# A decoder layer on one core: the opening loads in one queue, ten block pairs instead of eleven with two sums made by transfers, and another order in the ending

## The chip, the cores and the metric

The kernel runs on one core of one Trainium2 chip. The core has five engines that run side by side, each with its own instruction queue: TensorE (PE in the profile; PEld is its weight load), VectorE (DVE), ScalarE (ACT), GpSimd (POOL) and SyncE (SP). Transfers between the chip's memory (HBM) and the core's memory (SBUF) are issued from an engine's queue, mostly SP's, and are moved by 16 DMA engines. The metric is device microseconds from start to end of the program, the median of several runs.

## The reference

One layer of a decoder on 256 tokens of 2048 values, all in float32:

```python
h   = RMSNorm(x) * gain
qkv = h @ W_in                      # 2048 x 6144
a   = 8 heads stick-breaking attention, 8 heads rotary + dilated window attention
x   = x + RMSNorm(concat(normed heads) @ W_out)
u   = (RMSNorm(x) * gain) @ W_up    # 2048 x 11008
u   = causal depthwise convolution of width 3 over the tokens, + bias
y   = gelu(u[:, :5504]) * u[:, 5504:]
x   = x + RMSNorm(y @ W_down)       # 5504 x 2048
```

The weights are about 210 MB and are read once; 256 tokens are two token tiles of 128.

## The kernel before, in words

**Products in two parts.** TensorE multiplies a faster 32-bit type with fewer bits (`F32R`). To keep float32 accuracy, each operand is split into a high part (`wh`, a cast on ScalarE, line 88) and a low part (`wl`, a subtraction on VectorE, line 93), and a product is three matmuls: high x high, low x high, high x low. So each weight tile of 128 x 1024 costs a load on SP's queue, a cast on ScalarE, a subtraction on VectorE, and then matmuls. Raw tiles have five buffers (`RAW_BUFS`), high and low parts four each.

**Order.** The weights are a list of chunks in the order of use (values, queries and keys, output, up). For each chunk the main loop first issues loads two chunks ahead and splits one chunk ahead, then multiplies. The program is written in one order; a list scheduler then orders each engine's instructions by its own estimate of when operands are ready, ahead of time; on the chip every engine runs its list strictly in order. `pin(...)`, while `pinned[0]` is true, keeps an instruction in the written order.

**The opening (lines 219 to 242).** The first chunk of values has four blocks of 512 columns, each multiplied with one 128-row block of x transposed (`xT`). The weights come in three pieces of one, one and two blocks through SP's queue; the matching pieces of x come through ScalarE's queue (`load_x(lo, hi, nc.scalar)`, line 228), so these issues stand among ScalarE's casts. Later x blocks (four at a time) come through SP's queue. x is multiplied by its gain and split into `hT[0]` (high) and `hT[1]` (low). Before that, TensorE runs eight matmuls on zeros (`warm`, line 224).

**The up stage** ends with, for each of 43 blocks of 128 rows of y, the convolution and gate (`convolved`). Blocks of y are kept either as singles (`yt`) or, for pairs of neighbouring blocks, in the seven combinations that a 2 x 2 block product by Strassen's scheme in Winograd's form needs (`yp`).

**The down stage (class `Down`).** The output is made in two column halves of 1024. A single is a 128 x 1024 weight tile and takes 2 x 2 = 4 products (two token tiles, two column blocks of 512), each of three matmuls. A pair is two weight tiles, four blocks of 512 columns, and takes 7 products in place of 8. For it VectorE forms block sums: `T13` (one block added to both halves of the second tile, line 536, 128 x 1024), and `T24` (two sums of 128 x 512, lines 537 and 538). So a pair has four units: `T13`, `T24`, `Rb` (the second raw tile) and `Ra` (half the first). `_down_plan` lays the singles out: two, then each pair followed by some singles, four (`HELD`) at the end. `prepare` splits units three ahead of the one multiplied (`AHEAD`) and calls `load`, which issues tiles on SP's queue five ahead.

**Places.** `room`, a tile of four rows of 2048, reuses the place of `hT` (tag `hT`), so nothing may be written there before the last matmul of the up stage has read `hT`. It holds the output (`fg`), the last gain (`gbc`, a 1 MB broadcast load issued on SP's queue, line 806, and scaled on VectorE, line 807), and in `room[:, 3]` the sums `T13` and `T24`.

**The ending (`run`, lines 595 to 635).** The last four singles are multiplied bank by bank, and each bank is closed as it is complete: added into `fg` on VectorE (line 575), squared and summed on ScalarE (line 391), multiplied by the gain on VectorE or GpSimd (line 577). When a token tile's four sums of squares are there, `mean` and `newton` make its factor, and `put` (line 610) writes `fg * r + x` for some columns and issues their output transfer on SP's queue (line 611). The last bank is closed in two halves of 256 columns.

Of the kernel before, what the change touches and what calls it, by code (L numbers as in the profile page):

```python
# [16 lines left out]
P = 128  # L17
# [13 lines left out]

P_PRE, P_HEAD, P_FFN, P_CW, P_CB, P_END = 0, 16, 32, 48, 48 + 258, 48 + 258 + 86

NPAIR = 11
HELD = 4
PAIRS = [(FT // NPAIR * m, FT // NPAIR * m + 1) for m in range(NPAIR)]
SINGLES = [k for k in range(FT) if not any(k in pr for pr in PAIRS)]
# [14 lines left out]
def layer_kernel(ctx: ExitStack, tc: tile.TileContext, a, out: bass.AP):  # L52
# [12 lines left out]
    def pin(ins):  # L65

        if pinned[0]:
            tc.keep_in_program_order(ins)
        return ins
# [3 lines left out]
    def load(src, w, piece=HALF):  # L73
        raws = []
        for lo in range(0, w, piece):
            n = min(piece, w - lo)
            raw = wpool.tile([P, n], F32, tag="raw", name="raw", bufs=RAW_BUFS, padded_shape=[P, HALF])
            nc.sync.dma_start(raw, src[:, lo:lo + n])
            raws.append(raw)
        return raws  # L80

    def split(raws):

        return [low(raw, high(raw)) for raw in raws]

    def high(raw):
        wh = wpool.tile([P, raw.shape[1]], F32R, tag="wh", name="wh", bufs=4, padded_shape=[P, HALF])
        pin(A.copy(wh, raw))  # L88
        return wh
# [118 lines left out]
    def load_x(lo, hi, eng=nc.sync):  # L208
        eng.dma_start(xt[:, lo:hi, :], a["xT"][:, lo * S:hi * S].rearrange("p (k s) -> p k s", k=hi - lo))

    def split_x(lo, hi):

        for k in range(lo, hi):
            gp = gpre[:, k:k + 1]
            A.activation(hT[0][:, k, :], xt[:, k, :], AF.Copy, scale=gp)
            V.scalar_tensor_tensor(hT[1][:, k, :], xt[:, k, :], gp, hT[0][:, k, :].bitcast(F32), op0=ALU.mult, op1=ALU.subtract)
# [4 lines left out]
    warm = cpool.tile([P, 512], BF16, name="warm")  # L221
    V.memset(warm, 0.0)
    idle = ps_at.tile([P, 512], F32, tag="at", name="idle")
    for _ in range(8):
        T.matmul(idle, warm[:, 0:P], warm, start=True, stop=True)
    for lo, hi in ((0, 1), (1, 2), (2, 4)):
        raws[0] += load(chunks[0][3][:, lo * 512:hi * 512], (hi - lo) * 512)
        load_x(lo, hi, nc.scalar)
        if lo == 0:
            V.tensor_scalar(hT[0][:, 0, :], xt[:, 0, :], gpre[:, 0:1], None, op0=ALU.mult)  # L230
            parts_of[0] += split(raws[0][-1:])
            V.scalar_tensor_tensor(hT[1][:, 0, :], xt[:, 0, :], gpre[:, 0:1], hT[0][:, 0, :].bitcast(F32), op0=ALU.mult, op1=ALU.subtract)
        else:
            split_x(lo, hi)
            parts_of[0] += split(raws[0][-1:])
    nc.scalar.dma_start(ident, a["cst"][:, C_ID:C_END])
    for i in range(1, 4):
        load_x(4 * i, 4 * i + 4)
# [238 lines left out]
    class Down:  # L477
# [12 lines left out]
        ONE = ((4, 1, 0), (3, 0, 512), (2, 0, 0), (8, 1, 512))  # L490

        def __init__(self):
            self.units, self.tiles = [], []
            for cp in range(2):
                at = 0
                for kind, j in _down_plan(cp):
                    first = len(self.tiles)
                    n = 2 if kind == "pair" else 1
                    for _ in range(n):
                        self.tiles.append(a["w_dn"][cp, :, at:at + 1024])  # L500
                        at += 1024
                    if kind == "pair":
                        for what, prods in self.PAIR:
                            self.units.append((cp, what, j, first, prods))
                    else:
                        self.units.append((cp, "one", j, first, self.ONE))
            self.raws, self.parts, self.sums = [], [], {}
            self.left = {}
            for i, u in enumerate(self.units):
                for bank, _, _ in u[4]:  # L510
                    last = bank == 8 and i >= len(self.units) - HELD
                    for key in ((1, 8, 0), (1, 8, 256)) if last else ((u[0], bank),):
                        self.left[key] = self.left.get(key, 0) + 1
            self.begun = set()

        def load(self, n):
            while len(self.raws) < min(len(self.tiles), n):
                raw = wpool.tile([P, HALF], F32, tag="raw", name="raw", bufs=RAW_BUFS, padded_shape=[P, HALF])
                nc.sync.dma_start(raw, self.tiles[len(self.raws)])
                self.raws.append(raw)  # L520

        def prepare(self, n):
            while len(self.parts) < min(len(self.units), n):
                cp, what, j, first, _ = self.units[len(self.parts)]
                self.load(first + 5)
                ra = self.raws[first]
                if what == "one":
                    src = ra
                else:
                    rb = self.raws[first + 1]  # L530
                    if what == "T13":
                        t13, t24 = room[:, 3, 0:HALF], room[:, 3, HALF:]
                        self.sums = {"T13": t13, "T24": t24, "Rb": rb, "Ra": ra[:, 512:]}
                        b12 = ra[:, 0:512].rearrange("p (o c) -> p o c", o=1).broadcast_to([P, 2, 512])
                        two = lambda x: x.rearrange("p (o c) -> p o c", o=2)
                        V.tensor_tensor(two(t13), b12, two(rb), op=ALU.add)  # L536
                        V.tensor_tensor(t24[:, 0:512], t13[:, 0:512], rb[:, 512:], op=ALU.add)
# [41 lines left out]
        def run(self):  # L579
            n = len(self.units) // 2  # L580
            last_pair = max(u for u in range(n) if self.units[u][1] != "one")
            later = []
            for cp in range(2):
# [24 lines left out]
            def put(t, lo, hi, r):  # L608
                x = x1s[2 * t + lo // HALF][:, lo % HALF:(hi - 1) % HALF + 1]
                V.scalar_tensor_tensor(fg[:, t, lo:hi], fg[:, t, lo:hi], r, x, op0=ALU.mult, op1=ALU.add)  # L610
# [12 lines left out]
            take = self.close(1, 4)  # L623
            put(0, 1024, 1536, r)
            take(G)
            products(8, 0, 256)
            put(0, 1536, 2048, r)
            self.close(1, 8, 0, 256)(G)
            products(8, 256, 512)
            take = self.close(1, 8, 256, 512)  # L630
            mean = rows.mean(1, 5)
            take(V)
            r = rows.newton(*mean)
            for lo, hi in ((0, 1024), (1024, 1472), (1472, 1856), (1856, 2048)):
                put(1, lo, hi, r)

    down = Down()
# [245 lines left out]
```

## Time and profile before

| | us |
|---|---|
| median of 3 runs | 1136.12 (1135.79 to 1136.71) |
| profiled execution, its own time | 1135.25 |
| its span, from first to last instruction | 1133.2 |
| TensorE busy in the span | 1113.1 (98%) |
| VectorE busy | 864.1 (76%) |
| ScalarE busy | 647.1 (57%) |
| GpSimd busy | 6.1 (1%) |
| HBM read / written | 211.63 MB / 4.19 MB |

The profile is of one execution. Busy time of an engine is the time in which at least one of its instructions ran; matmuls overlap in a pipeline, so a busy TensorE may still wait a little between them. "Idle before, releaser" is what ended an engine's wait. A timeline row has the start, the duration, the engine, the line, the operation and its operands (written tile, arrow, read tiles); an engine's name with a q is its queue, which issues transfers. In rows of stretches the clock is the share of full speed that TensorE was granted, the DMA share is the mean busy share of the 16 DMA engines.

### The profile page before, as it was taken

Reading aid. Unit: us, or ns where it says so; the run is one execution under the profiler, and the core shown is the slowest. Engines: PE = TensorE matmul, PEld = TensorE weight load, DVE = VectorE, ACT = ScalarE, POOL = GpSimd, SP = SyncE. Lnnn points to the kernel's source line nnn. Section 1 sums busy time; section 2 is a strip of 40 time slices with the busy share of each in tenths; the row PEclk is TensorE's granted clock in tenths of the full one; section 3 lists DMA queues with packets and bytes.
Section 4 is the critical chain, followed back from the end, with each engine's and each line's share of the span. In section 5 each row is a group of like instructions: output and inputs, shape, how many; then the busy total and the mean of one; then the engine's idle time right before and its main releaser. Section 6 shows DMA issues by size and latency. Waiting matters only on the chain.

```text
span 1133.2 us, 16046 instructions
## 1 busy us (share of the span) xinstructions
PE 1113.1 (98%) x5866; PEld 944.1 (83%) x5866; DVE 864.1 (76%) x1350; ACT 647.1 (57%) x1041; POOL 6.1 (1%) x12
## 2 busy tenths in 40 slices
PE   8999999999999989999999999999999999999996
PEld 5888888888888878888888888888888878788775
DVE  6665565765765489888888888888787899999886
ACT  6565565655654386555555555555555556555553
POOL 0000000000000000000000000000000000000001
PEclk9999999999999999999999999999999999999999
DMA  9664545545556556555555556655555565565555
GB/s 343 246 218 154 185 151 171 172 158 183 158 168 195 189 187 205 186 186 186 189 186 190 186 186 190 190 186 188 186 188 186 154 220 202 187 211 197 186 204 204
DMA packets 59694, 216.86 MB, mean 191 GB/s; under 512 B 6752, under 2 KB 7648, under 8 KB 58848
## 3 DMA queue, kind: packets, MB, share of 16 engines
q1 hardware_dynamic: 58896, 215.25, 57.6%
q8 instruction: 46, 0.75, 0.3%
q10 hardware_dynamic: 720, 0.60, 0.2%
q14 instruction: 32, 0.26, 0.1%
HBM read 211.63 MB, written 4.19 MB: 190 GB/s over the span
## 4 chain that ended last, share of the span: by engine, by line
PE 94%; DVE 2%; ACT 1%; DMA 1%; issue 0%; DVEq 0%; SPq 0%; ACTq 0%
PE mmu L101 28%; PE mmu L104 14%; PE mmqk L101 11%; PE p L557 6%; PE p L555 6%; PE p L556 6%; PE mmqk L104 5%; PE mmo L138 3%; PE mmo L134 3%; PE mmv L135 3%; PE mmv L134 3%; PE mmo L135 3%; PE mmv L138 3%; DVE wl L93 1%; DMA mg<-in_xT 1%; PE mmu L111 1%
## 5 line engine op out<-in xcount | busy, mean ns | idle before, releaser
L93 DVE TENSOR_TENSOR wl<-raw,wh 128x1024 fp32r<-128x1024 f32 (+1 forms) x387 | 455.9, 1190 | 200.0 <-ACT wh L88 199.4
L88 ACT CAST wh<-raw 128x1024 fp32r<-128x1024 f32 (+1 forms) x387 | 391.4, 1023 | 336.4 <-PE mmu L101 193.9
L101 PE MATMUL mmu<-hT,wh 128*128 128x512 f32 x1344 | 340.6, 395 | 0.2 <-ACT wh L88 0.2
L101 PEld LDWEIGHTS mmu<-hT,wh 128*128 128x128 f32 x1344 | 240.8, 188 | 44.9 <-ACT wh L88 0.4
L104 PEld LDWEIGHTS mmu<-hT,wl 128*128 128x128 f32 x1344 | 184.1, 188 | 15.3
L104 PE MATMUL mmu<-hT,wl 128*128 128x256 f32 x1344 | 187.4, 282 | 0.0
L101 PE MATMUL mmqk<-hT,wh 128*128 128x512 f32 x512 | 132.8, 400 | 0.0
L101 PEld LDWEIGHTS mmqk<-hT,wh 128*128 128x128 f32 x512 | 91.9, 188 | 17.0
L88 ACT CAST wh<-room 128x1024 fp32r<-128x1024 f32 x44 | 46.2, 1051 | 80.4 <-DVE room L536 52.2
L104 PEld LDWEIGHTS mmqk<-hT,wl 128*128 128x128 f32 x512 | 70.0, 188 | 5.8
L104 PE MATMUL mmqk<-hT,wl 128*128 128x256 f32 x512 | 71.2, 281 | 0.0
L557 PE MATMUL p<-wl,yt 128*128 128x512 f32 (+1 forms) x172 | 66.7, 389 | 0.2 <-DVE wl L93 0.2
L555 PE MATMUL p<-wh,yt 128*128 128x512 f32 (+1 forms) x172 | 66.5, 387 | 0.0
L556 PE MATMUL p<-wh,yt 128*128 128x512 f32 (+1 forms) x172 | 66.4, 386 | 0.0
L557 PE MATMUL p<-wl,yp 128*128 128x512 f32 x154 | 60.7, 399 | 1.7 <-DVE wl L93 1.7
L555 PE MATMUL p<-wh,yp 128*128 128x512 f32 x154 | 60.7, 394 | 0.4 <-ACT wh L88 0.3
L556 PE MATMUL p<-wh,yp 128*128 128x512 f32 x154 | 60.4, 392 | 0.0
L93 DVE TENSOR_TENSOR wl<-room,wh 128x1024 fp32r<-128x1024 f32 x44 | 53.7, 1221 | 5.6 <-ACT wh L88 4.8
L134 PE MATMUL mmv<-wh,hT 128*128 128x512 f32 x128 | 52.1, 409 | 3.7 <-DVE hT L230 2.8
L449 ACT ACTIVATE cv<-u,par 128x256 f32<-128x256 f32 x86 | 51.4, 598 | 2.1 <-DVE u L447 2.1
L135 PE MATMUL mmv<-wh,hT 128*128 128x512 f32 x128 | 51.3, 401 | 0.0
L134 PE MATMUL mmo<-wh,mix 128*128 128x512 f32 x128 | 50.6, 396 | 0.0
(173 smaller groups left out, 1225.6 us busy)
## 6 DMA issues: line engine op xcount, KB each, us to landing
raw<-in_w_up SPq DMA_DIRECT2D x172, 512.0 KB, 4.1
raw<-in_w_dn SPq DMA_DIRECT2D x86, 512.0 KB, 4.3
raw<-in_w_qk SPq DMA_DIRECT2D x64, 512.0 KB, 3.8
raw<-in_w_o SPq DMA_DIRECT2D x32, 512.0 KB, 3.7
raw<-in_w_v SPq DMA_DIRECT2D x31, 512.0 KB, 3.7
x<-in_x SPq DMA_DIRECT2D x2, 1024.0 KB, 6.5
x_kept<-x SPq DMA_DIRECT2D x2, 1024.0 KB, 4.1
x1b<-x_kept SPq DMA_DIRECT2D x4, 512.0 KB, 5.9
```

Source lines behind the costliest of these rows:

```text
L88: pin(A.copy(wh, raw))
L93: pin(V.tensor_tensor(wl, raw, wh.bitcast(F32), op=ALU.subtract))
L101: T.matmul(ps, wh[:, j * P:(j + 1) * P], h[:, k, :, :], start=(k == 0), stop=False, skip_group_check=True)
L104: T.matmul(ps[:, 0, :], wl[:, j * P:(j + 1) * P], h[:, k, 0, :], start=False, stop=(k == KT - 1), skip_group_check=True)
L111: T.matmul(ps[:, 0, :], w[:, k % 8 * P:(k % 8 + 1) * P], h[:, k, 0, :], start=(k == 0 and w is parts[0][0]), stop=False, skip_group_check= ...
L134: T.matmul(ps[t], hi[:, k, tc_], ws, start=(first and i == 0 and j == 0), stop=False)
L135: T.matmul(ps[t], lo[:, k, tc_], ws, start=False, stop=False)
L138: T.matmul(ps[t], hi[:, k, tc_], wl[:, j * 512:(j + 1) * 512], start=False, stop=(last and i == len(parts) - 1 and j == n - 1))
L449: A.activation(cv, u, AF.Identity, scale=cw(2), bias=par[:, P_CB + f:P_CB + f + 1])
L555: T.matmul(ps, yh, wh[:, cs], start=key not in self.begun, stop=False)
L556: T.matmul(ps, yl, wh[:, cs], start=False, stop=False)
L557: T.matmul(ps, yh, wl[:, cs], start=False, stop=self.left[key] == 0)
```

## The change

1. **Opening.** The first two x blocks, and then the third and fourth, are loaded through SP's queue, between the three weight pieces, which stay as they were: weights, x, weights, x, weights. The first block's cast, VectorE's high part of x, its weights' low part and the low part of x are kept in this written order. Nine matmuls on zeros run in place of eight.
2. **Down.** Ten pairs instead of eleven, so 23 singles instead of 21. `T13` is no longer added on VectorE: its block `b12` is written twice side by side into a buffer by a broadcast load on SP's queue, and the pair's second tile is then added onto it, from HBM, by an accumulating transfer that GpSimd issues. There are two such buffers, in `room[:, 3]`; a third sum is not begun before the first has been taken. The loads of the sums begin only in `run`, up to ten units ahead of `prepare`. The first raw tile of a pair is loaded with its second half only. `T24` goes into another tile (the place of `pair` of the up stage); its two additions stay on VectorE.
3. **Ending.** The last 512 columns of the first token tile are written after both halves of the last bank are closed, and the last four output steps are 256, 768, 512 and 512 columns wide in place of 1024, 448, 384 and 192.
4. The memory for descriptors of such transfers is 4096 in place of 1024 bytes.

```diff
-NPAIR = 11
+NPAIR = 10
...
-    for _ in range(8):
+    for _ in range(9):
         T.matmul(idle, warm[:, 0:P], warm, start=True, stop=True)
-    for lo, hi in ((0, 1), (1, 2), (2, 4)):
-        raws[0] += load(chunks[0][3][:, lo * 512:hi * 512], (hi - lo) * 512)
-        load_x(lo, hi, nc.scalar)
...
+    w0 = chunks[0][3]
+    raws[0] += load(w0[:, 0:512], 512)
+    load_x(0, 2)
+    raws[0] += load(w0[:, 512:1024], 512)
+    load_x(2, 4)
+    raws[0] += load(w0[:, 1024:], 1024)
+    pinned[0] = True
+    wh0 = high(raws[0][0])
+    pin(V.tensor_scalar(hT[0][:, 0, :], xt[:, 0, :], gpre[:, 0:1], None, op0=ALU.mult))
+    parts_of[0].append(low(raws[0][0], wh0))
+    pin(V.scalar_tensor_tensor(hT[1][:, 0, :], xt[:, 0, :], gpre[:, 0:1], hT[0][:, 0, :].bitcast(F32), op0=ALU.mult, op1=ALU.subtract))
+    pinned[0] = False
+    split_x(1, 2)
+    parts_of[0] += split(raws[0][1:2])
+    split_x(2, 4)
+    parts_of[0] += split(raws[0][2:3])
...
+        def add(self, n):
+
+            while self.added < min(len(self.units), n):
+                cp, what, j, first, _ = self.units[self.added]
+                if what == "T13" and len(self.t13) == self.taken + 2:
+                    break
+                self.added += 1
+                if what == "T13":
+                    i = len(self.t13)
+                    t13 = room[:, 3, i % 2 * HALF:(i % 2 + 1) * HALF]
+                    b12 = self.b12[cp, j].rearrange("p (o c) -> p o c", o=1).broadcast_to([P, 2, 512])
+                    nc.sync.dma_start(t13.rearrange("p (o c) -> p o c", o=2), b12)
+                    G.dma_start(t13, self.tiles[first + 1], accum_op=ALU.add)
+                    self.t13[cp, j] = t13
...
                 self.load(first + 5)
+                if self.begun_sums:
+                    self.add(len(self.parts) + 10)
...
-                        V.tensor_tensor(two(t13), b12, two(rb), op=ALU.add)
+                        t13 = self.t13[cp, j]
+                        t24 = phB.tile([P, HALF], F32, tag="pair", name="t24", bufs=1)
+                        self.sums = {"T13": t13, "T24": t24, "Rb": rb, "Ra": ra}
                         V.tensor_tensor(t24[:, 0:512], t13[:, 0:512], rb[:, 512:], op=ALU.add)
-                        V.tensor_tensor(t24[:, 512:], t24[:, 0:512], ra[:, 512:], op=ALU.add)
+                        V.tensor_tensor(t24[:, 512:], t24[:, 0:512], ra, op=ALU.add)
+                        self.taken += 1
...
-            put(0, 1536, 2048, r)
             self.close(1, 8, 0, 256)(G)
             products(8, 256, 512)
             take = self.close(1, 8, 256, 512)
+            put(0, 1536, 2048, r)
             mean = rows.mean(1, 5)
             take(V)
             r = rows.newton(*mean)
-            for lo, hi in ((0, 1024), (1024, 1472), (1472, 1856), (1856, 2048)):
+            for lo, hi in ((0, 256), (256, 1024), (1024, 1536), (1536, 2048)):
                 put(1, lo, hi, r)
...
-    nc = bacc.Bacc("TRN2", target_bir_lowering=False, num_devices=1, dynamic_dma_scratch_size=1024)
+    nc = bacc.Bacc("TRN2", target_bir_lowering=False, num_devices=1, dynamic_dma_scratch_size=4096)
```

More of the change, by code (lines that the diff above doesn't have):

```diff
@@ L223, in layer_kernel @@
     idle = ps_at.tile([P, 512], F32, tag="at", name="idle")
-    for _ in range(8):
+    for _ in range(9):
         T.matmul(idle, warm[:, 0:P], warm, start=True, stop=True)
-    for lo, hi in ((0, 1), (1, 2), (2, 4)):
-        raws[0] += load(chunks[0][3][:, lo * 512:hi * 512], (hi - lo) * 512)
-        load_x(lo, hi, nc.scalar)
[L229 to L235, printed above, removed]
+    w0 = chunks[0][3]
[14 more added lines that the diff above has]
+    parts_of[0] += split(raws[0][2:3])
     nc.scalar.dma_start(ident, a["cst"][:, C_ID:C_END])
@@ L492, in __init__ @@
         def __init__(self):
-            self.units, self.tiles = [], []
+            self.units, self.tiles, self.b12, self.t13, self.added, self.taken, self.begun_sums = [], [], {}, {}, 0, 0, False
             for cp in range(2):
@@ L498, in __init__ @@
                     n = 2 if kind == "pair" else 1
-                    for _ in range(n):
-                        self.tiles.append(a["w_dn"][cp, :, at:at + 1024])
+                    for i in range(n):
+                        self.tiles.append(a["w_dn"][cp, :, at + (512 if n == 2 and i == 0 else 0):at + 1024])
+                        if n == 2 and i == 0:
+                            self.b12[cp, j] = a["w_dn"][cp, :, at:at + 512]
                         at += 1024
@@ L517, in load @@
             while len(self.raws) < min(len(self.tiles), n):
-                raw = wpool.tile([P, HALF], F32, tag="raw", name="raw", bufs=RAW_BUFS, padded_shape=[P, HALF])
-                nc.sync.dma_start(raw, self.tiles[len(self.raws)])
+                src = self.tiles[len(self.raws)]
+                raw = wpool.tile([P, src.shape[1]], F32, tag="raw", name="raw", bufs=RAW_BUFS, padded_shape=[P, HALF])
+                nc.sync.dma_start(raw, src)
                 self.raws.append(raw)
+        def add(self, n):
[11 more added lines that the diff above has]
+                    self.t13[cp, j] = t13
         def prepare(self, n):
@@ L582, in run @@
             later = []
+            self.begun_sums = True
             for cp in range(2):
```

4 lines of the change are left out of this document (removed).

## The prediction

> **What bounds the kernel now.** I read the page first, then busy time by stretches, then the timeline at both ends, then the groups of instructions of the down stage.
>
> ```profile
> span 1133.2 us, 16046 instructions
> PE 1113.1 (98%) x5866; PEld 944.1 (83%) x5866; DVE 864.1 (76%) x1350; ACT 647.1 (57%) x1041; POOL 6.1 (1%) x12
> ```
>
> TensorE is busy 98% of the span, so only three things can move the time: the 20 us in which it waits, the number of its matmuls, and waits that are new. The stretches (opening, middle, down, ending) show where it waits; columns are PE, PEld, DVE, ACT, POOL busy, granted clock, DMA share, GB/s:
>
> ```profile
> 0.00:13.00 13.00, 8.08 (x21) 3.83 (x21) 4.16 (x8) 4.55 (x7) 0.55 (x6) 0.87 0.83 290
> 13.00:895.60 882.60, 879.62 (x4868) 759.75 (x4869) 645.57 (x1104) 514.11 (x879) 0.69 (x2) 1.00 0.58 188
> 895.60:1123.30 227.70, 225.39 (x980) 180.47 (x978) 209.20 (x227) 126.79 (x149) 2.59 (x2) 1.00 0.57 197
> 1123.30:1133.20 9.90, 0.00 (x0) 0.00 (x0) 5.12 (x13) 1.63 (x8) 2.29 (x2) 0.76 0.53 199
> ```
>
> The middle is dense (879.6 of 882.6 us), so every microsecond won before it arrives at the end. In down VectorE is busy 92%: almost a second bound. The opening is a queue matter:
>
> ```profile
> 0.74 1.33 SPq L78 DMA_DIRECT2D raw<-in_w_v  x3
> 1.19 0.93 ACTq L209 DMA_DIRECT2D mg<-in_xT  x2
> 3.78 0.62 ACT L88 CAST wh<-raw 128x512 fp32r<-128x512 f32 x1 [1.76 <-DMA raw<-in_w_v]
> 5.80 0.34 ACTq L209 DMA_DIRECT2D mg<-in_xT  x1
> 7.05 0.35 DVE L230 TENSOR_SCALAR hT<-mg,gpre 128x256 fp32r<-128x256 f32 x1
> 7.55 0.71 PE L134 MATMUL mmv<-wh,hT 128*128 128x512 f32 x2 [2.76 <-DVE hT L230]
> 8.84 1.03 ACT L88 CAST wh<-raw 128x1024 fp32r<-128x1024 f32 x1
> 12.41 2.51 ACT L215 ACTIVATE hT<-mg,gpre 128x256 fp32r<-128x256 f32 x6 [2.54 <-DMA mg<-in_xT]
> 12.97 0.50 PE L134 MATMUL mmv<-wh,hT 128*128 128x512 f32 x1 [0.96 <-ACT hT L215]
> ```
>
> The first x block (128 KB, ScalarE's queue) is used at 7.05, although a weight piece twice its size was there at 3.78. The third x piece is issued only at 5.80, since its issue stands behind a cast that waits for weights; it is used at 12.41, and TensorE gets the third and fourth block of the first quarter only at 12.97. From there it is dense.
>
> **Part 1, the opening.** In one queue the pieces come in the order of use: 0.26 MB weights, 0.26 x, 0.26 weights, 0.26 x, 0.52 weights, then 0.52 x and 1.05 weights for the second quarter. What the DMA engines moved in this time before:
>
> ```profile
> 2.00:4.00 2.00, 2.00 (x6) 0.76 (x5) 0.00 (x0) 0.24 (x2) 0.00 (x0) 1.00 0.77 210
> 4.00:6.00 2.00, 0.79 (x2) 0.00 (x0) 0.69 (x1) 0.60 (x2) 0.00 (x0) 1.00 1.00 330
> 6.00:8.00 2.00, 0.45 (x2) 0.32 (x3) 1.44 (x3) 0.41 (x1) 0.00 (x0) 1.00 1.00 356
> 8.00:10.00 2.00, 2.00 (x8) 1.43 (x7) 0.58 (x2) 1.45 (x2) 0.00 (x0) 0.72 0.97 355
> 10.00:13.00 3.00, 2.04 (x6) 1.03 (x5) 1.18 (x2) 0.59 (x2) 0.00 (x0) 0.62 1.03 412
> ```
>
> I add up the last column: 0.42 MB by 4 us, 1.08 by 6, 1.79 by 8, 2.50 by 10. The first weights (0.26 MB) are in by 3.3 and were used at 3.78, so some 0.5 us pass from last byte to use. The first two x blocks (0.52 MB) are in at 4.3, usable at 4.8, scaled on VectorE in 0.35: first product at about 5.2 instead of 7.55. The bound is the 0.52 MB weight piece: 1.57 MB are in at 7.4, usable at 7.9, cast in 1.03: third block at 8.9 instead of 12.97. The second quarter's first piece (2.62 MB) is usable at 10.8 and cast by 11.8; the twelve matmuls begun at 8.9 need 2.8 us and about 0.3 for the low parts, so it is just in time, and later pieces come faster than TensorE takes them. Gain: 12.97 - 8.9 = **4.1 us**. Upper bound 5.0 (use 0.5 us sooner, and no wait for low parts); lower bound 1.8: those twelve matmuls at half clock, as the granted 0.50 to 0.72 between 8 and 13 us cost them before (2.3 us more). The ninth warm-up matmul ends by about 5.2, before the first product can start: nothing, or 0.4 us if x is earlier.
>
> **Part 2, the down stage: products.** Per column half, eleven pairs and 21 singles are 11x7+21x4 = 161 products of three matmuls; ten and 23 are 162. The rate, and what the stage should have taken:
>
> ```profile
> 895.62 0.39 PE L555 MATMUL p<-wh,yt 128*128 128x512 f32 x1
> 901.12 0.39 PE L555 MATMUL p<-wh,yp 128*128 128x512 f32 x1
> 1122.99 0.28 PE L557 MATMUL p<-wl,yt 128*128 128x256 f32 x1
> ```
>
> Eight products (24 matmuls) lie between the first two rows: 5.50 us, 0.229 per matmul. 322 products need 221.4 us; the stage takes 1123.27 - 895.62 = 227.65. So **6.2 us** are stalls, and two more products cost **1.4 us**. What the stalls wait for (idle before the matmuls of tile p and their weight loads), and VectorE's work per pair:
>
> ```profile
>   DVE wl L93: 8.9, 20
> L536 DVE TENSOR_TENSOR room<-raw 128x1024 f32<-128x1024 f32 x22 | 26.9, 1221 | 8.8 <-DMA raw<-in_w_dn 7.2 <-PE mmu L104 1.5
> L537 DVE TENSOR_TENSOR room<-room,raw 128x512 f32<-128x512 f32 x22 | 15.2, 689 | 0.6
> L93 DVE TENSOR_TENSOR wl<-room,wh 128x1024 fp32r<-128x1024 f32 x44 | 53.7, 1221 | 5.6 <-ACT wh L88 4.8
> ```
>
> It is VectorE being late with low parts. The change takes away L536 (26.9 us), and each of the two pairs that become singles saves two 689 ns sums, one 1221 ns low part and a half-width one (about 0.7): 3.3 us, 6.6 for both. VectorE falls from 209 to about 176 us of the stage. I keep 0.5 us of the stalls (0 to 3).
>
> **Part 2, the sums by transfer.** Each needs a broadcast through SP's queue and then an accumulating transfer issued by GpSimd, which the trace does not hold. In steady state they are hidden: two sums may be open, so one may start about two pair periods ahead: 2 x (7 + 1.7x4) products x 0.69 = 19 us. Against that stand:
>
> ```profile
> DMA to landing us min/median/max: 3.4/4.3/6.2
> room<-in_gpost SPq DMA_DIRECT2D x1, 1024.0 KB, 4.6
> 895.82 0.33 SPq L806 DMA_DIRECT2D room<-in_gpost  x1
> 900.00:904.00 4.00, 4.00 (x19) 3.30 (x18) 4.00 (x7) 3.10 (x6) 0.00 (x0) 1.00 0.01 2
> 901.90 1.22 DVE L807 TENSOR_SCALAR room<-room 128x2048 f32<-128x2048 f32 x1
> ```
>
> The first row is of down's 512 KB weight tiles. An accumulate has the same bytes and reads its destination too: at best 3.4, at worst twice 4.3 = 8.6; I take 5, nearer the plain row. Broadcast and accumulate are 9 to 15 us, under 19. The transfers add 20 x 0.79 MB = 70 GB/s (with destination reads 117) to the stage's 197, below the 412 seen at the start. SP's broadcast waits until a sum buffer is read; behind it stand weight loads, which wait for later low parts anyhow. GpSimd has nothing else to do until the ending.
>
> The **first** sum is not hidden. Its buffer lies in the tile that reuses the place of hT, free after the last up matmul at 895.6. SP first issues the 1 MB gain (895.82, landing 900.4), then the broadcast: its 0.52 MB follow at 412 GB/s, in by about 901.7. The accumulate ends at 906.7, the cast (1.05) at 907.8. TensorE's two singles end at 901.1; before, VectorE had made this sum by then. Uncovered that is 6.7 us; the pair's two other tiles (3 products, 2.1 us) and the next single (2.7 us) need no sum and can fill it if the order and buffers let them. I take **5.0 us**: the pair's own tiles fill 2.1, and 0.4 comes back as low parts that are late once more. Bounds: 0.3 (accumulate 3.4, all filled) and 10.3 (8.6, nothing filled).
>
> By the Trainium skill, "DMA: Bandwidth & Descriptors", section "Anatomy of one DMA", a transfer issued by GpSimd takes about 2.0 us plus its bytes at 436 GB/s, an estimate of 3.2 us here; the sum would end 1.8 us lower. Its "SBUF — State Buffer", "Who interferes with whom", speaks against the change: GpSimd cannot write descriptors while VectorE runs a two-port operation such as tensor_scalar. L807 is one, standing right where the first accumulate is issued; by that rule it is up to 1.2 us later, and the sum as much higher.
>
> Down in all: -6.2 + 0.5 + 1.4 + 5.0 = **+0.7 us**. The pair less in the up stage, and where its values lie, cost nothing: the middle is bound by TensorE.
>
> **Part 3, the ending.**
>
> ```profile
> 1122.66 1.41 DVE L610 SCALAR_TENSOR_TENSOR room<-room,rs,x1b 128x512 f32<-128x512 f32 x2
> 1123.98 0.75 DVE L575 TENSOR_TENSOR room<-p,room 128x256 f32<-128x256 f32 x2
> 1124.49 0.42 ACT L391 ACTIVATE jks<-room 128x256 bf16<-128x256 f32 x1 [0.99 <-DVE room L575]
> 1126.70 2.74 DVE L610 SCALAR_TENSOR_TENSOR room<-room,rs,x1b 128x1024 f32<-128x1024 f32 x4
> 1129.00:1132.00 3.00, 0.00 (x0) 0.00 (x0) 0.43 (x2) 0.00 (x0) 0.00 (x0) 0.50 0.88 326
> ```
>
> The last matmul ends at 1123.27, but VectorE is in the second 512-wide output step until 1124.07 and closes both last halves after it. Moved behind them, that step (0.7 us) runs while ScalarE squares: the chain starts 0.6 us sooner. The four last steps stay 2.74 us together; the small one first lets the output, whose 1 MB leaves at 326 GB/s until about 1131.6, begin some 0.8 us earlier, but the last issue stays at the end of the 2.74: 0.4. Gain **1.0 us** (0.3 to 1.5).
>
> **Sum.** -4.1 + 0.7 - 1.0 = -4.4 us on the profiled execution: 1135.25 to 1130.8. The median of the runs shown, 1136.12, is 0.87 above it: **1131.7 us**.
>
> **Rivals.** (a) The first sum is covered: everything ready is moved ahead and the accumulate is fast, 1 us of stall instead of 5: 1127.7. For it: ScalarE and VectorE have the raw tiles; against: the pair's casts come in order, and four buffers of high parts are shared. (b) Half clock in the opening: gain 1.8 instead of 4.1: 1134.0. For it the granted 0.50 to 0.72 of the rows above; against: with products from 5.2 on, TensorE has no pause like the one before 7.55. The Trainium skill, "TensorE: Matmul & The Clock Gate", "What's actually happening", has the clock set by free-running 3.4 us windows; the trace's low clock lasted about as long. (c) Slower: the accumulate itself takes 12 us. A buffer's round (5.3 broadcast, 12, 3 to cast and subtract) is then 20.3 us against 19 and every pair loses (20.3 - 19)/2, 13 us over twenty; the first sum stalls 12 instead of 5: 1131.7 + 13 + 7 = 1152. It decides from an accumulate of about 11 us; the first sum alone turns the total to loss at a stall of 9.4. For it: no row of its kind; against: a plain tile needs 6.2 at most. (d) The sums do not pay: VectorE freed, stalls stay at 6.2 because weights land later beside the added traffic: 1131.7 + 5.7 = 1137.4. For it, 7.2 us of waits of L536 on weights; against, 43% of the DMA engines free.
>
> **Chances.** Forecast 0.55, (a) 0.16, (b) 0.10, (c) 0.09, (d) 0.10. A measurement here can tell about 0.2%, 2.3 us. Forecast and (a), less a tenth whose first sum is slow, and a little of (b), are faster: 0.69; most of (b), that tenth and half of (d) are the same: 0.19; (c) and the rest of (d) slower: 0.12. The range from 1127.0 to 1138.0 takes in (a), (b) and (d) and leaves out (c). The forecast's own is 1129 to 1134.5.
>
> **What would show it.** First product near 5.2, third block near 8.9, clock 1.0 through 13 us. In down one wait of about 5 us after the first two singles, ended by ScalarE's cast of a sum released by an accumulating transfer, and later waits on L93 nearly gone. Ending about 9 us after the last matmul. Wrong if sums keep being waited for beyond the first pair, or if the opening is still ended by x.

## The result, and the profile after

The changed kernel takes 1148.43 us (median of 4, 1146.44 to 1149.23), the kernel before, run beside it on the same chip, 1135.95: a ratio of 1.0112 (95% interval 1.0097 to 1.0127). It is 12.5 us slower; 1131.7 was forecast. The profiled execution took 1149.23, its span is 1147.1.

The page's busy times of the changed kernel:

```profile
span 1147.1 us, 16136 instructions
PE 1118.3 (97%) x5873; PEld 948.0 (83%) x5873; DVE 834.3 (73%) x1316; ACT 646.6 (56%) x1037; POOL 23.8 (2%) x32
```

VectorE lost 30 us of work, where 33.5 were worked out; TensorE waits 9 us longer in all and is busy 5 us longer. Where, is told by the same four stretches as before (PE, PEld, DVE, ACT, POOL busy, granted clock, DMA share, GB/s):

```profile
0.00:13.00 13.00, 10.40 (x33) 5.67 (x33) 6.30 (x13) 7.58 (x12) 0.84 (x7) 1.00 0.81 287
13.00:893.00 880.00, 876.84 (x4859) 756.57 (x4858) 642.28 (x1095) 510.54 (x874) 0.52 (x1) 1.00 0.58 188
893.00:1136.10 243.10, 231.07 (x986) 185.73 (x984) 179.70 (x197) 126.89 (x145) 20.02 (x22) 0.97 0.85 251
1136.10:1147.10 11.00, 0.01 (x1) 0.00 (x0) 6.03 (x13) 1.61 (x8) 2.40 (x2) 0.68 0.48 180
```

Down starts at 893.0 instead of 895.62 (2.65 us won), lasts 243.1 instead of 227.7 (15.4 lost), and the ending takes 11.0 instead of 9.9 (1.1 lost): 13.9 together, which is 1147.1 - 1133.2. In down the DMA share rose from 0.57 to 0.85, for 251 GB/s instead of 197.

The opening, rows of the timeline:

```profile
5.66 1.19 PE L134 MATMUL mmv<-wh,hT 128*128 128x512 f32 x2 [0.45 <-ACT hT L215]
9.13 1.04 ACT L88 CAST wh<-raw 128x1024 fp32r<-128x1024 f32 x1 [1.71 <-DMA raw<-in_w_v]
10.23 0.50 PE L134 MATMUL mmv<-wh,hT 128*128 128x512 f32 x1 [0.95 <-ACT wh L88]
```

The first product starts at 5.66 (7.55 before), the third block at 10.23 (12.97 before). The clock is 1.00 through 13 us. The third block now waits for the cast of the weight piece of two blocks, which landed at 9.1; 7.9 was forecast.

The start of down, the same view (a queue's row groups issues, so its duration isn't that of one):

```profile
893.15 0.33 SPq L832 DMA_DIRECT2D room<-in_gpost  x1
893.53 14.94 SPq L542 DMA_DIRECT2D room<-in_w_dn  x3
897.78 0.39 PE L580 MATMUL p<-wh,yt 128*128 128x512 f32 x1
897.99 1.23 DVE L833 TENSOR_SCALAR room<-room 128x2048 f32<-128x2048 f32 x1 [0.51 <-DMA room<-in_gpost]
899.97 1.92 POOL L543 DMA_DIRECT2D room<-in_w_dn  x2 [867.31 <-DMA room<-in_w_dn]
905.52 1.04 ACT L88 CAST wh<-room 128x1024 fp32r<-128x1024 f32 x1 [7.20 <-DMA room<-in_w_dn]
906.62 0.79 PE L580 MATMUL p<-wh,yp 128*128 128x512 f32 x1 [7.99 <-ACT wh L88]
907.92 2.51 ACT L88 CAST wh<-raw 128x1024 fp32r<-128x1024 f32 x3
909.57 0.63 PE L580 MATMUL p<-wh,yp 128*128 128x512 f32 x1
911.73 0.40 PE L580 MATMUL p<-wh,yp 128*128 128x512 f32 x1
```

The chain is gain load, broadcast (issued 893.53, landed 899.3), accumulate (issued 899.97, landed 905.5), cast. TensorE's two singles are used up at 898.4, and it waits 8.2 us. Nothing fills the gap: ScalarE casts the pair's raw tiles only at 907.92, behind the sum. And TensorE comes back at half clock, with matmuls of 0.63 us instead of 0.40 until about 911:

```profile
906.00:912.00 6.00, 5.38 (x14) 3.90 (x15) 5.97 (x7) 4.32 (x6) 0.00 (x0) 0.56 0.65 154
912.00:940.00 28.00, 28.00 (x124) 22.98 (x123) 20.70 (x22) 15.58 (x17) 2.57 (x3) 1.00 0.98 277
940.00:1000.00 60.00, 55.95 (x232) 43.98 (x231) 43.05 (x46) 30.57 (x32) 5.17 (x6) 0.97 0.92 266
1000.00:1050.00 50.00, 50.00 (x216) 40.51 (x215) 41.23 (x47) 28.74 (x36) 3.45 (x4) 1.00 0.86 259
```

Wait and half clock together are 10.6 us more than the matmuls until 912 need at 0.229 each (1.1 before). From 912 to 1000 the DMA engines are busy 92 to 98% of the time, and yet they move only 266 to 277 GB/s; in the opening they moved 412 at a share of 1.03. Between 912 and 1000 TensorE loses another 7.3 us (1.7 before). What one of the later waits hangs on, in two rows of the timeline:

```profile
984.46 0.69 DVE L561 TENSOR_TENSOR t<-room,raw 128x512 f32<-128x512 f32 x1 [4.83 <-DMA raw<-in_w_dn]
986.34 0.79 PE L582 MATMUL p<-wl,yt 128*128 128x512 f32 x1 [2.19 <-DVE wl L93]
```

TensorE waits for a low part, VectorE is late with it because it waited 4.83 us for a raw weight tile. So VectorE is no longer late of itself: it stands before weights that land late. The page's transfers (issues, KB each, median us to landing; and the share of 16 engines' span by queue, q0 being GpSimd's):

```profile
q1 hardware_dynamic: 64624, 221.02, 58.1%
q0 software_dynamic: 2880, 10.49, 5.1%
raw<-in_w_dn SPq DMA_DIRECT2D x66, 512.0 KB, 4.6
room<-in_w_dn SPq DMA_DIRECT2D x20, 512.0 KB, 5.7
room<-in_w_dn POOLq DMA_DIRECT2D x20, 512.0 KB, 7.5
raw<-in_w_dn SPq DMA_DIRECT2D x20, 256.0 KB, 5.8
```

Twenty accumulates occupy 5.1% of 1147.1 us of all 16 engines: 2.9 us each. The plain queue's 221 MB take 58.1%, which is 1.6 us per 512 KB. A half tile of 256 KB now needs 5.8 us to land; a whole one needed 4.3 before.

The end, timeline:

```profile
1136.11 0.42 DVE L600 TENSOR_TENSOR room<-p,room 128x256 f32<-128x256 f32 x1
1136.37 2.40 POOL L602 TENSOR_TENSOR room<-room 128x512 f32<-128x512 f32 x2 [2.97 <-ACT jks L397]
1136.44 1.73 DVE L636 SCALAR_TENSOR_TENSOR room<-room,rs,x1b 128x512 f32<-128x512 f32 x1
1138.10 0.41 DVE L600 TENSOR_TENSOR room<-p,room 128x256 f32<-128x256 f32 x1
```

The moved output step does not stand behind both closes: the scheduler put it between them, and beside GpSimd's two multiplies it takes 1.73 us instead of 0.74 (its like at 1135.45). The second close starts at 1138.10, some 1.7 us behind the place that the step took.

### The profile page after: what moved, and what is told of

Same layout as the page of the kernel before. It is cut to its first block, busy times and chain, and to the rows that moved or that the text cites. A ratio compares the mean times of both kernels' runs of the same rounds, so it can differ in the third digit from the quotient of the medians.

```text
span 1147.1 us, 16136 instructions
## 1 busy us (share of the span) xinstructions
PE 1118.3 (97%) x5873; PEld 948.0 (83%) x5873; DVE 834.3 (73%) x1316; ACT 646.6 (56%) x1037; POOL 23.8 (2%) x32
## 3 DMA queue, kind: packets, MB, share of 16 engines
q1 hardware_dynamic: 64624, 221.02, 58.1%
## 4 chain that ended last, share of the span: by engine, by line
PE 91%; DMA 4%; DVE 2%; ACT 1%; issue 1%; SPq 0%; DVEq 0%; ACTq 0%; POOLq 0%
PE mmu L101 27%; PE mmu L104 14%; PE mmqk L101 10%; PE p L582 5%; PE mmqk L104 5%; PE p L580 5%; PE p L581 5%; PE mmo L138 3%; PE mmv L134 3%; PE mmo L134 3%; PE mmo L135 3%; PE mmv L138 3%; PE mmv L135 3%; DMA room<-in_w_dn 2%; DMA raw<-in_w_dn 1%; DVE wl L93 1%
## 5 line engine op out<-in xcount | busy, mean ns | idle before, releaser
L88 ACT CAST wh<-raw 128x1024 fp32r<-128x1024 f32 (+1 forms) x387 | 395.8, 1026 | 365.8 <-PE mmu L101 194.5
L104 PEld LDWEIGHTS mmu<-hT,wl 128*128 128x128 f32 x1344 | 182.8, 189 | 15.2
L582 PE MATMUL p<-wl,yt 128*128 128x512 f32 (+1 forms) x188 | 74.7, 398 | 3.5 <-DVE wl L93 3.4
L581 PE MATMUL p<-wh,yt 128*128 128x512 f32 (+1 forms) x188 | 74.0, 394 | 0.0
L580 PE MATMUL p<-wh,yt 128*128 128x512 f32 (+1 forms) x188 | 74.0, 393 | 0.0
L580 PE MATMUL p<-wh,yp 128*128 128x512 f32 x140 | 56.3, 402 | 8.0 <-ACT wh L88 8.0
L582 PE MATMUL p<-wl,yp 128*128 128x512 f32 x140 | 56.3, 402 | 0.6 <-DVE wl L93 0.6
L581 PE MATMUL p<-wh,yp 128*128 128x512 f32 x140 | 56.1, 401 | 0.0
L134 PE MATMUL mmo<-wh,mix 128*128 128x512 f32 x128 | 50.6, 396 | 0.0
L135 PE MATMUL mmo<-wh,mix 128*128 128x512 f32 x128 | 50.0, 390 | 0.0
L582 PEld LDWEIGHTS p<-wl,yt 128*128 128x128 f32 x188 | 35.8, 191 | 13.1 <-DVE wl L93 5.5
```

What stands on the lines that cost most here:

```text
L104: T.matmul(ps[:, 0, :], wl[:, j * P:(j + 1) * P], h[:, k, 0, :], start=False, stop=(k == KT - 1), skip_group_check=True)
L134: T.matmul(ps[t], hi[:, k, tc_], ws, start=(first and i == 0 and j == 0), stop=False)
L135: T.matmul(ps[t], lo[:, k, tc_], ws, start=False, stop=False)
L580: T.matmul(ps, yh, wh[:, cs], start=key not in self.begun, stop=False)
L581: T.matmul(ps, yl, wh[:, cs], start=False, stop=False)
L582: T.matmul(ps, yh, wl[:, cs], start=False, stop=self.left[key] == 0)
```

## The experiments

Those on the kernel before add one part at a time; those on the changed kernel take one thing away or replace it. A ratio is to the kernel before, timed beside the run, with its 95% interval. "Stalls" are the time of down beyond 0.229 us per matmul of 512 columns (0.1175 per matmul of 256), the tail is what follows the last matmul.

**The opening alone.** Before, with part 1 of the diff.

> The kernel before with part 1 (the opening) alone. Theory A (parts add up; the trace of the changed kernel has the third block at 10.23 instead of 12.97 and the down stage beginning 2.65 us earlier): 2.7 us faster, 1133.3 us. Rival (the opening only moves a wait to a later place, and the earlier start of down was owed to the pair less): no difference, 1136 us. The 4.1 us of the prediction would need the third block at 8.9.

Measured 1133.50 us, ratio 0.9986 (0.9977 to 0.9995): 1.6 us won. Rows of its timeline:

```profile
9.89 0.50 PE L134 MATMUL mmv<-wh,hT 128*128 128x512 f32 x1 [0.85 <-ACT wh L88]
14.38 0.50 PE L134 MATMUL mmv<-wh,hT 128*128 128x512 f32 x1 [1.42 <-ACT wh L88]
```

The third block came at 9.89, and the second quarter waited another 1.4 us for its first cast (13.30 to 14.34): its weight piece landed only at 12.9, and ScalarE's x work kept the cast waiting another 0.4. So the third block comes as early as theory A has it, and a part of the gain is handed back at the second quarter.

**Ten pairs alone.** Sums on VectorE as before:

```diff
-NPAIR = 11
+NPAIR = 10
```

> The kernel before with ten pairs instead of eleven, all block sums on VectorE. Theory A: two more products cost 1.4 us, VectorE has about 9 us less work in down, so that some 2 to 3 of the 6.2 us of stalls go: 1135.0 us. Rival (the stalls come from places that one pair less does not touch): 1137.5 us.

Measured 1133.32, ratio 0.9984 (0.9974 to 0.9994), where I had expected 1135. What ended TensorE's waits in down (us, times; 8.9 in 20 times before):

```profile
  DVE wl L93: 3.6, 8
```

One pair less in each column half takes 5.3 of the 8.9 us of waits for low parts: 6 matmuls more (1.4 us), stalls down from 6.4 to 3.1.

**The ending alone.** Before, with part 3.

> The kernel before with part 3 (the ending) alone. Theory A (the moved output step lands between the two closing halves and collides with GpSimd's multiplication, 1.73 us instead of 0.74 in the changed kernel's trace): 1.1 us slower, 1137.1 us. Rival (the prediction: the squares begin sooner): 1.0 us faster, 1135.0 us.

Measured 1135.73, ratio 1.0005 (0.9995 to 1.0014): no difference that can be told, between the two theories. The tail in its trace is 10.3 us against 9.9.

**The sums and ten pairs, no other part.** Before, with part 2.

> The kernel before with part 2 alone (ten pairs, the sums by transfer); opening and ending as before. Theory A (down itself loses 15.5 us: about 10.7 at the first sum, and later stalls): 1151 us, with one wait of about 8 us before the first pair. Rival (the loss needs the earlier start or the moved ending): under 1141 us.

Measured 1150.19, ratio 1.0130 (1.0115 to 1.0146). So the loss is all in part 2, and as ten pairs alone win 2, the transfers cost 17. The first wait in its trace is 8.2 us again, and the stalls between 912 and 1000 are there too (5.9).

**Six singles first.** The changed kernel; the first sum gets four singles' time more:

```diff
-    plan = [("one", left.pop(0)) for _ in range(0 if cp else 2)]
+    plan = [("one", left.pop(0)) for _ in range(0 if cp else 6)]
```

> The changed kernel with six singles ahead of the first pair instead of two (the weights laid out to match), so that TensorE has 16.5 us of work while the first sum is made. Theory A (the wait of 8.2 us is the uncovered first sum, and the 2.5 us behind it are the half clock that the pause causes): both vanish, some 7.5 us of later stalls stay: 1137.7 us. Rival (the transfers cannot keep up, the wait only moves to the first or second pair): over 1144 us.

Measured 1147.91, ratio 1.0104 (1.0089 to 1.0120); the rival held. The first wait is 2.2 us instead of 8.2, but the stalls between 912 and 1000 grow from 7.3 to 15.2. One of these, in its timeline:

```profile
951.97 0.50 PE L582 MATMUL p<-wl,yt 128*128 128x512 f32 x1 [2.38 <-DVE wl L93]
```

The plan has fewer singles left between the pairs, so the later sums follow each other faster. The time is owed to something that all the sums share.

**No accumulate.** The changed kernel without GpSimd's transfer (the sum then is its first block alone):

```diff
-                    G.dma_start(t13, self.tiles[first + 1], accum_op=ALU.add)
```

> The changed kernel without the accumulating transfers: the sum is only the broadcast block, so the products of the sums are of other numbers; SP's issues and all waits for the broadcast stay. Theory B (later stalls come from DMA engines that are 92 to 98% busy because an accumulate takes more of them than its bytes): later stalls fall from 7.5 to under 2 us, the first wait to about 2.7: 1135 us. Rival C (the later stalls come from SP's queue, where weight loads stand behind a broadcast that waits for its buffer): they stay, 1140 us.

Measured 1131.79, ratio 0.9966 (0.9953 to 0.9979). Its stretches:

```profile
912.00:940.00 28.00, 28.00 (x125) 22.95 (x123) 23.54 (x25) 16.24 (x18) 0.00 (x0) 1.00 0.71 233
940.00:1000.00 60.00, 60.00 (x264) 49.23 (x263) 47.57 (x50) 34.93 (x37) 0.00 (x0) 1.00 0.77 243
```

Theory B held. From 912 on TensorE never waits, and the DMA engines are busy 71 to 77%. All that is left, 4.3 us, lies at the first pair, whose broadcast alone comes too late. So all stalls after 912 come from the accumulates; that VectorE was the bound, and is relieved, holds. It also bounds the change as it stands: even with accumulates that cost nothing it is no faster than the 1131.35 below. What sums without the wait at the first pair, and without the new ending, could reach was not run.

**Broadcast from GpSimd's queue.** To tell a full SP queue from full DMA engines:

```diff
-                    nc.sync.dma_start(t13.rearrange("p (o c) -> p o c", o=2), b12)
+                    G.dma_start(t13.rearrange("p (o c) -> p o c", o=2), b12)
```

> The changed kernel with the broadcast issued by GpSimd, like the accumulate, instead of by SP, so that no weight load stands behind it. Rival C (SP's queue): later stalls fall from 7.5 to about 2 us, 1143 us. Theory B (DMA engines full): they stay or grow, 1148 to 1152 us; the first sum is then about 1 us later, since GpSimd has two descriptors to write.

Measured 1147.69, ratio 1.0100 (1.0082 to 1.0118); first wait 8.5 us, 7.2 us between 912 and 1000, as in the changed kernel. It isn't the queue. Nor does GpSimd, while it issues an accumulate, slow VectorE: in the changed kernel's trace a low part of 128 x 1024 takes 1.22 us beside such an issue as without one.

**A plain second transfer.** The changed kernel; GpSimd's transfer overwrites instead of adding:

```diff
-                    G.dma_start(t13, self.tiles[first + 1], accum_op=ALU.add)
+                    G.dma_start(t13, self.tiles[first + 1])
```

> The changed kernel, with GpSimd's second transfer a plain one that overwrites what the broadcast wrote: the same 512 KB on the same queue to the same place, but nothing is added, so that the sum lacks the first block. Theory B1 (it is the adding that makes the transfer dear: 2.9 us of all 16 DMA engines against about 1.6 us for a plain 512 KB): the DMA share of 940 to 1000 us falls from 0.92 to 0.75 to 0.85, the 7.6 us of later stalls shrink to under 3, the first wait of 8.2 us by 1 to 3; 1139 to 1143. Rival B2 (a second 512 KB transfer on GpSimd's queue costs as much, whatever it does): share over 0.9, first wait and later stalls stay, 1146 to 1150.

Measured 1142.35, ratio 1.0060 (1.0046 to 1.0074). The page's transfers and the stretches:

```profile
q0 software_dynamic: 2880, 10.49, 2.5%
room<-in_w_dn POOLq DMA_DIRECT2D x20, 512.0 KB, 6.1
```

```profile
912.00:940.00 28.00, 28.00 (x124) 22.99 (x123) 22.54 (x25) 16.29 (x17) 1.58 (x3) 1.00 0.83 290
940.00:1000.00 60.00, 58.10 (x248) 47.18 (x247) 43.23 (x45) 32.67 (x35) 3.17 (x6) 0.97 0.83 277
```

The same packets and bytes take 2.5% of the engines instead of 5.1: it is the adding that doubles the price (1.4 us of all 16 engines each, against 2.9). The start of down shows it with little else in flight, first in the changed kernel, then here; from 901 on the first two of these transfers run alone:

```profile
901.00:908.00 7.00, 1.38 (x3) 0.83 (x3) 2.45 (x3) 2.08 (x3) 0.89 (x1) 0.50 0.86 150
901.00:905.00 4.00, 0.02 (x1) 0.02 (x1) 1.08 (x2) 1.04 (x1) 0.35 (x1) 0.50 0.76 262
```

Both rows are 1.05 MB; accumulating takes 6.0 us of all engines (7.00 x 0.86) for it, overwriting 3.0. More bytes move per second at a lower share (0.83). In the run without adding, the first wait shrinks to 6.8 us, the stalls between 912 and 1000 from 7.3 to 3.7, a little more than the 3 that I had allowed. The adding costs 0.0052 of the time, 5.9 us; that a second transfer is there at all, against none, costs 0.0094, 10.7 us; in the traces 5.3 of it lie before 912, at the first pair, and 3.9 between 912 and 1000. B1 held, its 1139 to 1143 too.

**First sum on VectorE.** The changed kernel; the very first pair's sum (`near` is true for `cp == 0 and j == 0`) as before the change:

```diff
+                        if self.near(cp, j):
+                            b12 = ra[:, 0:512].rearrange("p (o c) -> p o c", o=1).broadcast_to([P, 2, 512])
+                            V.tensor_tensor(two(t13), b12, two(rb), op=ALU.add)
+                            ra = ra[:, 512:]
```

> The changed kernel, with the very first pair's first sum made by VectorE from the pair's two tiles as before, and the other nineteen by the transfers. Theory A (the first sum's price is the 8.2 us of waiting and the 2.5 us at half clock behind it, and nothing else in down depends on it): down's stalls fall from 20.4 to 8 to 11 us, 1137 to 1140. Rival B (the DMA engines are full from the first transfers on, so the wait moves to the second pair or to the weights): stalls stay above 14 us, 1143 to 1149.

Measured 1141.07, ratio 1.0050 (1.0035 to 1.0065): 7.0 us better than the changed kernel, 1.07 us over theory A's range and below rival B's; the stalls fall to 10.6, inside A's range. Those until 912 fall from 10.6 to 3.1 us, those from 912 to 1000 stay (7.0). Rows of its timeline:

```profile
946.42 0.69 DVE L573 TENSOR_TENSOR t<-room,raw 128x512 f32<-128x512 f32 x1 [3.96 <-DMA raw<-in_w_dn]
948.30 0.50 PE L594 MATMUL p<-wl,yt 128*128 128x512 f32 x1 [1.32 <-DVE wl L93]
```

The two losses are separate: a first sum that nothing covers, and weights that land late beside nineteen accumulates.

**Opening and ten pairs.** Before, with part 1 and `NPAIR = 10`; neither transfers nor new ending.

> The kernel before with the opening and ten pairs, all sums on VectorE, and the ending as before: parts 1 and the cheap half of 2. Theory A (gains add: 0.14% and 0.16% alone): ratio 0.9970, 1131.9 us. Rival (an earlier start of down meets the same late VectorE work, so one gain eats the other): 0.9985, 1133.5 us.

Measured 1131.35, ratio 0.9958 (0.9942 to 0.9975). The gains add (0.9986 times 0.9984 is 0.9970, inside the interval), and this kernel beats both.

**Every other sum by transfer.** The same kernel, where `near`, the test for a sum that stays on VectorE, is true for even pairs, and one sum by transfer is open at a time:

```diff
+            return j % 2 == 0
...
+                if far and len(self.t13) == self.taken + 1:
```

> The opening's new order and ten pairs, the ending as before; of each column half the even pairs' first sums stay on VectorE, the odd pairs' come by the broadcast and the accumulating transfer, so that one such sum is open at a time and the first pair has none. Theory A (transfers can carry some sums at no price as long as the DMA engines keep room): half the accumulates take the DMA share of down from 0.64 to 0.80 without them to some 0.75 to 0.90, no wait at the first pair, and the 3.8 us of stalls in down with ten pairs on VectorE (1131.35 us) fall to 1 to 2.5 us: 1129.0 to 1130.5. Rival B (each transfer sum takes more from the weights' landing than it gives VectorE): stalls of 4 to 8 us, 1131.5 to 1136.

Measured 1132.97, ratio 0.9977 (0.9968 to 0.9986): my theory fell. Its stretch and what ended TensorE's waits:

```profile
940.00:1000.00 60.00, 60.00 (x264) 49.25 (x263) 48.40 (x51) 32.88 (x35) 2.56 (x3) 1.00 0.82 261
```

```profile
  DVE wl L93: 4.6, 9
  ACT wh L88: 2.9, 5
```

At a share of 0.82 little is lost between 912 and 1000 (0.3 us), but the stalls of down are 5.2 us in all against 3.8 without transfers; the difference of 1.4 us lies before 912, at the first sum that comes by transfer. So half as many win nothing: the time is no better than without transfers, by the middle values 1.6 us worse, with ratios whose intervals overlap.

**The ending kept in its order.** The kernel with opening and ten pairs, and part 3, with VectorE's work of the ending pinned:

```diff
+            pinned[0] = True
...
+            pin(V.tensor_tensor(dst, self.ps[(bank,) if hi - lo == 512 else (bank, lo)], dst, op=op))
```

> The opening's new order, ten pairs on VectorE, and the change's ending, with VectorE's closes, squares and output steps of the ending kept in the order in which they are written, so that no output step comes between the two closing halves. Theory A (the ending lost by the place that the scheduler gave the moved step): the tail from the last matmul falls from the 10.0 us of the same kernel with the old ending to 9.0 to 9.5, 1130.3 to 1130.9. Rival B (the step beside GpSimd's two multiplies takes 1.7 instead of 0.74 us wherever it stands): tail 10.0 to 10.6, 1131.3 to 1132.

Measured 1130.70, ratio 0.9958 (0.9945 to 0.9970), the same ratio as without part 3. Rows of its timeline:

```profile
1120.68 0.75 DVE L581 TENSOR_TENSOR room<-p,room 128x256 f32<-128x256 f32 x2
1120.94 2.39 POOL L583 TENSOR_TENSOR room<-room 128x512 f32<-128x512 f32 x2 [2.96 <-ACT jks L397]
1121.34 1.40 DVE L616 SCALAR_TENSOR_TENSOR room<-room,rs,x1b 128x512 f32<-128x512 f32 x1
1122.67 0.15 DVE L407 TENSOR_SCALAR_CACHE_REDUCE rj<-ssd 128x5 f32<-128x5 f32 x1
```

Both halves are now closed early, but the step still stands beside GpSimd and takes 1.40 us. The last square is there at 1122.24, the reduction on VectorE starts at 1122.67, after the step. The time lies in theory A's range, but the tail is 9.7 us against 10.0, between the theories' figures: the place was one fault, the collision another, and what the order can win, 0.3 us, is less than can be told.

## Why the prediction was wrong

In the terms of the forecast, for the profiled execution (forecast 1130.8, measured 1149.23, 18.4 apart):

| term | forecast | measured |
|---|---|---|
| opening | -4.1 | -2.65 |
| two more products | +1.4 | +1.4 |
| stalls of down before | -6.2 | -6.4 |
| first sum | +5.0 | +10.6 |
| other stalls kept in down | +0.5 | +7.3 |
| slower matmuls from 988 on | none | +2.5 |
| ending | -1.0 | +1.1 |

The stalls of before are the same in both columns; 6.4 counts 0.229 us per matmul, 6.2 the 5.50 us per 24.

**The step "the first sum is not hidden" had its mechanism right and its size wrong.** Gain load, broadcast and accumulate came in the order and nearly with the times worked out (accumulate 5.5 us, 5 assumed; the sum was in at 905.5, 906.7 forecast, though down began 2.7 sooner). Three things failed. Counted from the start of down, the sum was in after 12.5 us, where 11.1 were forecast. "The pair's own tiles fill 2.1" did not happen: ScalarE casts in order, and the sum's cast stands first. And the wait was costed at its own length; behind a pause of 8.2 us come some 4.5 us at half clock, 2.5 us more, although the rows of the opening before, with a clock of 0.62 to 0.72 after a pause, showed it. The run with the first sum on VectorE puts both at 7.0 us in timed runs.

**The step "in steady state they are hidden" is the larger error in kind.** It compared the length of one sum with its lead, which came out (behind the first pair ScalarE waited for a sum once more, 1.5 us), and the load by bytes ("70 GB/s, with destination reads 117, to the stage's 197, below the 412"). Bytes weren't what ran out: at 266 to 277 GB/s the engines were 92 to 98% busy. An accumulate takes 2.9 us of all 16 engines where a plain transfer of the same size on the same queue takes 1.4, shown by the plain second transfer. Rival (d), stalls that stay because weights land later beside the added traffic, was this mechanism. I gave it 0.10 and priced it at the stalls of before, "against, 43% of the DMA engines free": that is the share before the change; 20 accumulates of 2.9 us, 20 broadcasts, less 20 halves of tiles, fill it, as the rows from 912 on show. Rival (c), an accumulate of 12 us, came near in time (1152) for another reason: landing takes 5.5 to 9.0, so that its nearness is luck.

By the Trainium skill, "DMA: Bandwidth & Descriptors", section "Anatomy of one DMA", the accumulate was estimated at 3.2 us; the trace has 5.5 to 9.0, so the measurement decides against that estimate. The lock of GpSimd that "SBUF — State Buffer", "Who interferes with whom", would have set here decided nothing: the first accumulate was issued at 899.97, 0.6 us after the broadcast had landed, and L833 had ended at 899.22, before that landing.

**VectorE as the second bound was right**, and the run without accumulates shows it: no stall after 912. But ten pairs alone already took half of that gain (stalls 6.4 to 3.1), which the forecast saw only as 6.6 us less of VectorE's work. What was left for the transfers to win was about 3 us.

**The opening** won less, 2.65 us in this trace and 1.6 when timed alone. The step that failed is "1.57 MB are in at 7.4": it lets the queue's pieces end strictly one after the other. The stretches of the changed kernel:

```profile
2.00:4.00 2.00, 2.00 (x6) 0.76 (x5) 0.00 (x0) 0.01 (x1) 0.00 (x0) 1.00 0.84 241
4.00:6.00 2.00, 1.55 (x4) 0.52 (x3) 0.84 (x2) 1.24 (x3) 0.30 (x1) 1.00 0.92 312
6.00:8.00 2.00, 2.00 (x8) 1.25 (x8) 2.00 (x6) 1.41 (x3) 0.00 (x0) 1.00 0.98 321
8.00:10.00 2.00, 1.27 (x6) 0.69 (x4) 0.39 (x1) 0.87 (x1) 0.00 (x0) 1.00 0.93 346
```

By 8 us they add up to 1.75 MB, near the 1.79 of before, so the rate held; 1.57 MB were in at 7.4 as worked out. But the cast of the weight piece began at 9.13, 1.2 us after the 7.9. By then, at the last row's rate, some 2.1 MB had been moved, so about half a megabyte of them were of pieces behind it, although the pieces landed in the order of issue (4.3, 5.1, 5.9, 6.5, 9.1 and 10.4 us in this trace). What lets later pieces move before an earlier one is whole stays open; no run tested it. The lower bound, 1.8, held for the trace, and not for the reason given (the clock was 1.00).

**The ending** failed at "moved behind them, that step runs while ScalarE squares": the written order isn't the scheduled one, and GpSimd's multiplies stand in the same stretch. By the Trainium skill, "SBUF — State Buffer", "Who interferes with whom", a VectorE instruction with two SBUF inputs contends with a GpSimd instruction that reads SBUF; the trace agrees (0.74 us alone, 1.73 and 1.40 beside it), and I had not used it here.

## What to carry to other kernels

Before work is moved from a compute engine to the DMA engines, cost it in time of these engines, not in bytes, and measure that time for the kind of transfer: an accumulate took twice a plain one. A sum with a long lead in steady state still has a first one; ask what covers that, and add the half clock behind a long pause of TensorE. And time the parts alone first: here two small ones won 0.4% together, and the idea that they came with lost 1.5%.

## What was not expected of the hardware

An accumulating transfer of 512 KB from HBM onto SBUF kept the DMA engines busy for 2.9 us of all 16 and landed after 5.5 to 9.0 us; a plain one on the same queue took 1.4 us and landed after 4.0 to 7.5.

In the down stage of the changed kernel's profile the matmuls of 512 columns follow each other at 0.229 us until the wait at 984 to 988, and at 0.2333 from there to the end, at a granted clock of 1.00 in both: 216 instead of 220 are counted in the 50 us from 1000, and to the end it costs 2.5 us. In every kernel's trace the matmuls of the output product (320 to 390 us) follow each other at 0.229, and those before it and in the up stage at 0.233; in down only this execution has 0.233, and other kernels with waits as long (2.1 us at 990 with the plain second transfer) do not. What sets it stays open; as it was seen in a single profile, which is the slowest of the four timed executions, it is no cost of the change that can be counted on.
